# One load of x issued ahead of one load of addends, in a matmul kernel that streams its tiles

## Chip, cores and metric

The kernel runs on one core of a Trainium2 chip. The metric is the device time of one execution in microseconds (us), given as the median over several runs. The profile and the trace belong to one further execution, whose instructions and transfers the hardware profiler recorded.

## What is computed

```python
# x 16 x 512 x 1024, weight 1024 x 768, add_value 16 x 512 x 768, all float32; scale = 0.1
def reference(x, weight, scale, add_value):
    return (scale * np.matmul(x, weight) + add_value).astype(np.float32)
```

The 16 x 512 rows of x are one run of 8192 rows, that is 64 tiles of 128 rows. Each tile is multiplied by the same weight, scaled, and added to its tile of addends.

## The kernel before

**Data.** A group is eight tiles, and a partition of the chip holds eight neighbouring rows of a group, so that a load of four tiles of x brings 16 KB and a load of four tiles of addends 12 KB to each partition in one piece. `xs` has room for 16 tiles of x in float32 (a ring of four blocks of four tiles, one semaphore for each block: `x0` to `x3`). `ao` has room for 32 tiles: addends are loaded into it, the result is written over them, and the stores to `out` read it from there. The weight comes in through `ao` at the start and is kept as `w_bf` in bf16.

**Transfers.** All of them are issued by SyncE (SP) and go through one queue, in the order of the list `STREAM` (lines 19 to 25). An entry `("x", 56, 4)` loads four tiles of x from tile 56 on, `"a"` loads addends, `"w"` weights, and `"o"` stores results. `sync_engine` (lines 84 to 129) walks the list and puts a wait ahead of an entry only where it is needed, and only if no earlier wait on that semaphore was as strict (`need`, line 87):

- a load of x waits until ScalarE and GpSimd have cast the tiles that were in its place in the ring (lines 99 to 102);
- a load of addends that begins a group waits for the earlier such loads (line 109), and one into a place that held results waits for the store of these (line 114);
- a load of addends that begins in the middle of a group (tiles 52 to 55 are the only such load) signals `a_late`; all others signal `a_sem` (lines 116 to 120);
- a store waits for its results (`made`, line 125), and for the store two before it (line 124).

The last group of results (tiles 56 to 63, `LAST`) is stored by line 224, after all five engines have met at the end of the block that line 217 opens.

**Casting.** `mover` (lines 131 to 145) runs on ScalarE (ACT) and on GpSimd (POOL). For each block of four tiles it waits for the load, and for a free `va` buffer of the two, and then each engine makes eight casts of 32 partitions from `xs` to `va` (line 144). Blocks are taken in order.

**VectorE (DVE).** `group` (lines 172 to 179) is VectorE's fixed order for eight tiles. It mixes two kinds of work: `finish` takes the products of two tiles out of PSUM, scales them, adds the addends and leaves the result in `ao` (line 168); `turn` transposes half a cast block in 32 x 32 squares from `va` to `xt` (line 159). For tiles 48 to 55 the order is: wait for the addends of tiles 48 to 51; finish 48, 49; turn the first half of the block of tiles 52 to 55; finish 50, 51; turn its second half; **wait for `a_late`**; finish 52, 53; turn the first half of the block of tiles 56 to 59, which waits for all its casts; finish 54, 55; turn its second half. In the code:

```python
                if p == 2 and not last:
                    eng.wait_ge(a_late, i)
                finish(p, at, i + (4 * p - 12) if p < 3 else i)
                if p < 2 or not last:
                    turn(1 if p < 2 else 0, p % 2, i + 8 if p == 2 else i)
```

**TensorE (PE).** `tensor_engine` (lines 201 to 215) takes the tiles in order, sixteen matmuls a tile (eight slices of the contraction, each for 512 and 256 columns), into four PSUM places. Ahead of each pair of tiles it waits for their half block in `xt` and for the PSUM places to be finished.

## Time and profile before

The median of three runs is 212.03 us (211.53 to 212.54). The profiled execution took 212.22 us; its span, from the first to the last recorded instruction, is 210.2 us, and some 2.0 us lie around it.

| | busy us | share of the span | instructions |
|---|---|---|---|
| TensorE, matmuls (PE) | 170.3 | 81% | 1008 |
| TensorE, weight loads (PEld) | 50.8 | 24% | 512 |
| VectorE (DVE) | 97.9 | 47% | 66 |
| ScalarE (ACT) | 134.7 | 64% | 129 |
| GpSimd (POOL) | 135.4 | 64% | 132 |
| DMA queue | share of 16 engines 97.0% | 87.03 MB, mean 414 GB/s | 4720 packets |

The granted TensorE clock is 0.968 on average over the span. The DMA share is that of 16 DMA engines which work side by side: 1.00 says that all of them moved data all the time. A load or a store counts as landed when the last of the 16 engines has done its part. "Idle before" with an arrow names what ended an engine's wait. All stretches are in microseconds from the start of the span.

### The profile page before, as it was taken

What the parts mean: (1) busy time and instruction counts of PE and PEld (TensorE: products, weight loads), DVE (VectorE), ACT (ScalarE), POOL (GpSimd) and SP (SyncE); (2) the same over time, 40 slices, a digit from 0 to 9 for tenths busy, and PEclk for the clock granted to TensorE, in tenths of its full rate; (3) what the DMA queues carried; (4) which work ended last, traced back from release to release, by engine and by line L of the source; (5) the groups of instructions that cost most, each with busy time, mean ns of one, the idle gap of its engine ahead of it and who ended that gap; (6) DMA issues with size and microseconds to landing.
All of it is one profiled execution on the core that took longest, in us unless ns stands there. A gap on an engine that the chain in (4) does not pass through costs nothing.

```text
span 210.2 us, 2215 instructions
## 1 busy us (share of the span) xinstructions
PE 170.3 (81%) x1008; PEld 50.8 (24%) x512; DVE 97.9 (47%) x66; ACT 134.7 (64%) x129; POOL 135.4 (64%) x132
## 2 busy tenths in 40 slices
PE   0000999999999999999999999999998946999700
PEld 0000222223322223322223322223322211233200
DVE  0045245465537555555555555553719307155310
ACT  2492957995599999996950999379940599600000
POOL 0398956995599999997960899379950599700000
PEclk9999999999999999999999999999999995999985
DMA  6999999999999999999999999999999999999577
GB/s 231 407 447 447 412 426 424 449 449 399 455 443 399 424 474 399 449 426 412 435 421 437 451 421 441 418 426 449 402 426 433 430 449 430 416 430 444 234 299 299
DMA packets 4720, 87.03 MB, mean 414 GB/s; under 512 B 496, under 2 KB 496, under 8 KB 1008
## 3 DMA queue, kind: packets, MB, share of 16 engines
q1 hardware_dynamic: 4720, 87.03, 97.0%
HBM read 61.87 MB, written 25.17 MB: 414 GB/s over the span
## 4 chain that ended last, share of the span: by engine, by line
DMA 63%; POOL 15%; PE 11%; issue 2%; SPq 2%; DVE 1%; POOLq 0%; DVEq 0%
DMA xs<-in_x_dram 29%; DMA out_dram<-ao 27%; POOL va L144 15%; PE mm L193 11%; DMA ao<-in_add_value_dram 7%; DVE ao L168 1%; SPq L115 1%; DVE xt L159 1%; SPq L105 1%; SPq L96 0%; POOLq L137 0%; SPq L104 0%; POOLq L139 0%; SPq L89 0%; DVEq L157 0%
## 5 line engine op out<-in xcount | busy, mean ns | idle before, releaser
L193 PE MATMUL mm<-w_bf,xt 128*128 128x256 bf16 (+1 forms) x1008 | 170.3, 330 | 28.1 <-DVE xt L159 27.3
L144 POOL CAST va<-xs 32x1024 bf16<-32x1024 f32 x128 | 135.2, 1056 | 47.1 <-DMA xs<-in_x_dram 38.8
L144 ACT CAST va<-xs 32x1024 bf16<-32x1024 f32 x128 | 133.4, 1043 | 46.6 <-DMA xs<-in_x_dram 41.5
L168 DVE SCALAR_TENSOR_TENSOR ao<-mm,ao 128x1536 f32 (+1 forms) x32 | 56.2, 1755 | 75.6 <-PE mm L193 70.4
L191 PEld LDWEIGHTS <-xt 128*128 128x128 bf16 x512 | 50.8, 99 | 147.2 <-issue 118.3
L159 DVE STREAM_TRANSPOSE xt<-va 128x1024 f32<-128x1024 f32 x32 | 39.5, 1235 | 13.3 <-POOL va L144 13.3
L152 DVE CAST w_bf<-ao 128x3072 bf16<-128x3072 f32 x2 | 4.5, 2248 | 13.5 <-DMA ao<-in_weight_dram 13.5
L133 ACT ACT_TABLE_LOAD x1 | 1.3, 1283 | 0.9 <-SPq L217 0.9
L241 POOL MEMSET const-float32-0.0<- 128x1 f32 x1 | 0.1, 98 | 0.2 <-issue 0.2
L241 POOL MEMSET const-bfloat16-1.0<- 128x1 bf16 x1 | 0.1, 100 | 0.0
L241 POOL MEMSET const-float32-1.0<- 128x1 f32 x1 | 0.1, 98 | 0.0
L241 POOL MEMSET const-uint8-127<- 128x1 uint8 x1 | 0.1, 98 | 0.0
## 6 DMA issues: line engine op xcount, KB each, us to landing
out_dram<-ao SPq DMA_DIRECT2D x8, 3072.0 KB, 29.1
ao<-in_add_value_dram SPq DMA_DIRECT2D x7, 3072.0 KB, 17.1
xs<-in_x_dram SPq DMA_DIRECT2D x8, 2048.0 KB, 20.9
xs<-in_x_dram SPq DMA_DIRECT2D x4, 4096.0 KB, 23.1
ao<-in_weight_dram SPq DMA_DIRECT2D x2, 1536.0 KB, 12.3
ao<-in_add_value_dram SPq DMA_DIRECT2D x2, 1536.0 KB, 12.8
```

The lines of the kernel that those rows point to most:

```text
L105: move = eng.dma_start(xs[:, k:k + n, :], rows(x_v, s, n))
L115: move = eng.dma_start(ao[:, slot(s):slot(s) + n, :], rows(add_v, s, n))
L133: eng.preload_act_table(mybir.ActivationFunctionType.Copy)
L144: copy(va[q % VA_BUFS][32 * b:32 * b + 32, :, a, :], src[32 * a:32 * a + 32, :, b, :]).then_inc(count, 1)
L152: eng.tensor_copy(w_bf[:, s:s + n, :], ao[:, s:s + n, :]).then_inc(casts, n)
L159: eng.transpose(xt[:, 2 * half:2 * half + 2, :, :].rearrange("p i c m -> p (i c m)"), va[move % VA_BUFS][:, q:q + 2 * KC, :, :].bitcast(fp ...
L168: eng.scalar_tensor_tensor(a, mm[:, q:q + 2, 0:N], float(scale), a, op0=mybir.AluOpType.mult, op1=mybir.AluOpType.add).then_inc(made, 2)
L191: eng.ldweights(x_j, tile_position=(0, 0))
L193: m = eng.add_instruction(mybir.InstMatmult(start_tensor_calc=(j == 0), stop_tensor_calc=(j == KJ - 1), tile_size=(P, P), tile_position=(0 ...
L241: nc = _bacc.Bacc("TRN2", target_bir_lowering=False, num_devices=1)
```

## The change

One entry of the list moves ahead by one place. No instruction is added or removed.

```diff
@@ -20,8 +20,8 @@
     ("a", 24, 8), ("x", 32, 8), ("o", 0, 8), ("o", 8, 8), ("a", 32, 8), ("x", 40, 4),
-    ("x", 44, 4), ("a", 40, 8), ("x", 48, 8), ("o", 16, 8), ("o", 24, 8), ("a", 48, 4), ("a", 52, 4),
-    ("x", 56, 4), ("x", 60, 4), ("a", 56, 8), ("o", 32, 8), ("o", 40, 8), ("o", 48, 8),
+    ("x", 44, 4), ("a", 40, 8), ("x", 48, 8), ("o", 16, 8), ("o", 24, 8), ("a", 48, 4), ("x", 56, 4),
+    ("a", 52, 4), ("x", 60, 4), ("a", 56, 8), ("o", 32, 8), ("o", 40, 8), ("o", 48, 8),
 ]
 LAST = (56, 8)
```

In the built program only SyncE's order differs. Before, from the load of the addends of tiles 48 to 51 on: addends 48 to 51 (waits for the store of tiles 16 to 23), addends 52 to 55, x 56 to 59 (waits for casts), x 60 to 63 (waits for casts), addends 56 to 63, three stores. After: addends 48 to 51, x 56 to 59 (waits for casts), addends 52 to 55, x 60 to 63 (waits for casts), and the rest as before. The instructions of the other four engines, and their waits, are the same.

## The prediction

> **What bounds the kernel now.** I read the DMA share first, because 97.0% of 16 engines is the highest share on the page, and ask where the missing part is. The stretches of the last 45 us show it (columns: stretch, its length, busy time of PE, PEld, DVE, ACT, POOL with counts, granted clock, DMA share, GB/s):

> ```profile
> 170.40:172.50 2.10, 0.01 (x1) 0.00 (x0) 0.00 (x0) 2.05 (x3) 1.98 (x3) 1.00 1.01 433
> 172.50:175.40 2.90, 0.00 (x0) 0.00 (x0) 1.23 (x2) 2.83 (x4) 2.72 (x4) 0.54 0.95 407
> 175.40:179.70 4.30, 4.23 (x14) 1.06 (x8) 2.81 (x3) 4.20 (x5) 4.06 (x5) 0.51 1.05 452
> 179.70:196.20 16.50, 16.42 (x101) 4.95 (x51) 7.57 (x5) 2.50 (x3) 2.97 (x3) 1.00 1.00 429
> ...
> 197.30:198.00 0.70, 0.70 (x7) 0.20 (x3) 0.00 (x0) 0.00 (x0) 0.00 (x0) 1.00 0.10 35
> 198.00:198.50 0.50, 0.45 (x4) 0.00 (x0) 0.00 (x0) 0.00 (x0) 0.00 (x0) 1.00 0.12 49
> 198.50:201.00 2.50, 0.00 (x0) 0.00 (x0) 1.76 (x1) 0.00 (x0) 0.00 (x0) 1.00 0.00 0
> 201.00:208.90 7.90, 0.00 (x0) 0.00 (x0) 0.00 (x0) 0.00 (x0) 0.00 (x0) 0.66 0.93 398
> ```

> The queue is full until about 197.3, then nearly empty until 201, and then it moves the last store alone. So the hole of some 3.7 us ahead of the last store is all that the end of the kernel can give back. Next, the chain of waits (start, duration, what) says why the last store is late:

> ```profile
> 146.61 18.50 DMA xs<-in_x_dram
> ...
> 165.34 1.03 POOL va L144
> ...
> 174.17 1.26 DVE xt L159
> ...
> 175.47 10.30 PE mm L193 x50
> ...
> 198.56 1.76 DVE ao L168
> ```

> The load of x 56 to 59, issued at 146.61, lands at 165.1. Its casts, its transpose, the last eight tiles on TensorE and the last finish follow without a pause, and the store is issued at 200.60. The timeline shows TensorE's pause in it, and VectorE's order around that pause:

> ```profile
> 159.83 10.57 PE L193 MATMUL mm<-w_bf,xt 128*128 128x512 bf16 x63 [0.81 <-DVE xt L159]
> 175.47 22.98 PE L193 MATMUL mm<-w_bf,xt 128*128 128x512 bf16 x126 [5.07 <-DVE xt L159]
> 165.35 1.76 DVE L168 SCALAR_TENSOR_TENSOR ao<-mm,ao 128x1536 f32 x1 [2.79 <-PE mm L193]
> 174.17 1.25 DVE L159 STREAM_TRANSPOSE xt<-va 128x1024 f32<-128x1024 f32 x1 [7.06 <-POOL va L144]
> 156.92 28.19 SPq L126 DMA_DIRECT2D out_dram<-ao  x3
> ```

> TensorE ends tile 55 at 170.40 and starts tile 56 at 175.47. The finish of tiles 52 and 53 at 165.35, which needs the moved addends, waited for TensorE and not for them. (In the last row SyncE issues three stores, the third at 184.8, once the first has landed.)

> **The transfers one by one.** The rows of DMA issues, taken in stretches that hold one or two issues, give times to landing: addends 48 to 51, 11.2 us from 145.36, so 156.5; addends 52 to 55, 14.5 from 145.74, so 160.2; x 56 to 59, 165.1; x 60 to 63, 22.5 (the two x loads have a mean of 20.5, the first 18.5) from about 147.4, so 170.0; addends 56 to 63, 20.8 from 156.54, so 177.3; the stores of tiles 32 to 39 and 40 to 47, 27.8 and 34.8, so 184.7 and 192.2; the store of 48 to 55, 14.9 from 184.8, so 199.7. They land in the order of issue: a 3072 KB transfer takes 7.3 to 7.5 us of the ladder, x 4.9, the small addends 3.7.

> **The change, step by step.**

> *SyncE.* The same two DMAs swap places. The pair of addends took 1.15 us to issue, the pair of x 1.56, so x 56 is issued some 0.8 us earlier and addends 52 as much later. Both still stand in the queue behind the store of tiles 24 to 31 and addends 48, which land at 156.5, so this costs 0; without that cover it would be 0.8. The wait for casts that now comes ahead of addends 52 is for tiles 40 to 47 at most. POOL's timeline has its last 32 casts (tiles 48 to 63) from 138.00 on and the ones before ended at 133.5, 12 us before SyncE comes by: 0. What is queued behind it (x 60, addends 56, three stores) keeps its place, with the same bytes ahead.

> *x 56 to 59* lands behind addends 48 alone: 156.5 + 4.9 = 161.4 instead of 165.1, 3.7 earlier. From landing to TensorE's start took 175.47 - 165.11 = 10.36 (eight casts and a transpose). ACT and POOL are idle from 155.5 on, and VectorE has ended the finish of 52 and 53 by 167.1, so tile 56 starts at 161.4 + 10.4 = 171.8. TensorE's pause falls from 5.07 to 1.4.

> *Addends 52 to 55* land where x 56 did, at 165.1 (the sum of the bytes is the same), 4.9 later than before. Finish 52 needs them at 165.35, so the stall is 0 to 0.2. Behind that finish in VectorE's order stands the transpose of tile 56, which cannot start before its casts end at 170.4; the finish takes 1.76, so addends up to 168.4 cost nothing. Without that cover each microsecond is one.

> *x 60 to 63* lands at 170.0 as before. Its casts, so far hidden behind those of x 56 until 174.05, can now start at 170.4, take another 8.7 and end at 179.1. TensorE wants tile 60 four tiles (two finishes 5.2 apart, 188.16 to 193.36) after 171.8, at 182.2. With 1.3 for the transpose, 1.8 us are spare.

> *The clock.* The profile shows 1.00 after a pause of 0.81 us and about 0.5 from 172.7 to 179.7 around the pause of 5.07: the first pair of the last eight took 7.4 us, the later pairs 5.2. A pause of 1.4 lies between these rows, so 0 to 2.2 us can come on top of the 3.7. It is nearer the row of 0.81; but I carry both, since the last store is issued at 200.60 - 3.69 = 196.9 with the slow stretch, and at 194.7 without. [...]

> *The end.* Neither decides, because of the DMA queue. It has the same bytes to move before the last store: the store of tiles 48 to 55 is released by the landing at 184.7, which the swap does not touch, and lands at 199.7. Though most engines have done it by 198, 0.12 of 16 engines for 0.5 us at 198.0 to 198.5 is one engine with one more packet (a row counts a packet where it begins), and the last store cannot land before that engine has done its share of it too. Queued without a gap, it lands one more step of the ladder later: 199.7 + 7.5 = 207.2. Before it was 200.60 + 8.7 = 209.3. **Gain 2.1 us**, not 3.7. The condition is an issue before the late engine runs dry, at 199.2: with the 0.7 to 0.9 us from issue to first packet (issue at 200.60, none in 200.50 to 201.25, the first by 201.50) by 198.3. So 1.4 us are spare in the worse clock case, 3.6 in the better.

> **Sum.** Span 210.2 - 2.1 = 208.1, and with the same 2.0 around it 210.1 for the profiled execution. That one stood 0.19 above the median, so the forecast is 212.03 - 2.1 = **209.9 us**. Steps of 7.3 to 7.5 and the spread of the runs (0.5 to either side) give it a range of its own of 209.2 to 210.7.

> **Rivals.**

> *All of TensorE's gain comes through (chance 0.10).* If no engine is late on the store of 48 to 55, the last store starts at 197.5 and not at 201.3, the gain is 3.7, and the time 208.3. For it: the share is 0.10 already from 197.3 to 198.0. Against: the 0.12 after that, and the landing at 199.7.

> *The meeting of the engines waits for the store of 48 to 55 (0.08).* In the trace its landing, 199.7, comes before VectorE's end, 200.3, so it may be a hidden condition of line 224. Then the issue falls from 200.6 only to 199.7 + 0.3 = 200.0, a gain of 0.6: 211.4. Against: the list of SyncE's waits names VectorE alone there, and the code has no wait for these stores.

> *Slower: the addends of 52 come out of their turn (0.05).* Place: the wait for `a_late` in VectorE's order, ahead of the transpose that TensorE waits for. From the row of addends 48 (landing 156.5, finish 156.86, next transpose 158.54, TensorE 159.83), a landing at L starts tile 56 at L + 3.3. It decides from L = 168.5, the end moves when L passes 169.9, and above 172.2 the kernel is slower, one for one. With x 60 (170.0) nearly all the gain would remain; with addends 56 (177.3) tile 56 starts at 180.6, 5.1 late: 217.1. Against: every landing in the ladder is in order. [...]

> *The load does not come earlier (0.04).* If x 56 lands at 165.1 wherever it stands, nothing moves: 212.0. Against: the ladder again, where each transfer's step fits its bytes.

> **How the numbers follow.** My forecast has 0.73. About 0.5% (1.06 us) is what a measurement of this kernel can tell from no change, so faster means under 210.97: 0.72 of the forecast and the first rival, 0.82; the second, the fourth and a little of the forecast make 0.13 the same; 0.05 slower. The range reaches towards the first rival and down to a gain of 0.9: 208.6 to 211.1.

> **What would show it.** After: x 56 lands near 161.4 and TensorE's last pause is 1 to 2 us; the clock around it is 1.00, or dips; the finish of 52 still starts at 165.3 to 165.6; the third store is issued near 184.8; line 224 issues between 194 and 197.5; the DMA share has no hole ahead of the last store, whose time to landing grows from 8.7 to 10 or more; the end is near 208. Wrong would be: a last issue that waits for a landing, a VectorE wait on addends beyond 168, or a hole in the DMA share elsewhere.

## The result, and the profile after

The changed kernel takes 209.86 us (median), the kernel before beside it 212.41: a ratio of 0.9881, 95% interval 0.9854 to 0.9908, or 1.2% faster. One of the six runs of the changed kernel took 330.97 us at a mean granted clock of 0.566, for a reason that no run shows; the ratio leaves it out, and the median of the other five (209.78 to 209.94, clock 0.972 to 0.977) is 209.80. The profiled execution took 209.79 us, with a span of 207.7 us (before 212.22 and 210.2).

The issues of the two loads that changed places, from the rows of DMA issues (size, time to landing), in their new order:

```profile
xs<-in_x_dram SPq DMA_DIRECT2D x1, 2048.0 KB, 15.7
```

```profile
ao<-in_add_value_dram SPq DMA_DIRECT2D x1, 1536.0 KB, 18.5
```

Issued at 145.74 and 146.60, they land at 161.4 and 165.1; before, it was 165.1 and 160.2. The timeline of the changed kernel (start, duration, instruction; in brackets the idle time before it and what ended it):

```profile
171.77 20.98 PE L193 MATMUL mm<-w_bf,xt 128*128 128x512 bf16 x126 [1.37 <-DVE xt L159]
165.34 1.76 DVE L168 SCALAR_TENSOR_TENSOR ao<-mm,ao 128x1536 f32 x1 [2.79 <-PE mm L193]
170.47 1.25 DVE L159 STREAM_TRANSPOSE xt<-va 128x1024 f32<-128x1024 f32 x1 [3.36 <-POOL va L144]
177.37 1.76 DVE L168 SCALAR_TENSOR_TENSOR ao<-mm,ao 128x1536 f32<-128x1536 f32 x1 [2.87 <-DMA ao<-in_add_value_dram]
156.91 28.22 SPq L126 DMA_DIRECT2D out_dram<-ao  x3
194.89 0.33 SPq L224 DMA_DIRECT2D out_dram<-ao  x1
```

TensorE's pause ahead of tile 56 has gone from 5.07 to 1.37 us, and its last eight tiles run in 20.98 instead of 22.98. The finish of tiles 52 and 53 starts at 165.34 as before (165.35), so the later addends cost nothing there. Line 224 issues the last store at 194.89, 5.7 us earlier than before. Of these 5.7 the span has kept 2.5. The stretches show where the rest went (stretch, length, busy time of PE, PEld, DVE, ACT, POOL, granted clock, DMA share, GB/s):

```profile
170.40:172.50 2.10, 0.73 (x5) 0.29 (x3) 2.04 (x2) 2.05 (x3) 2.04 (x2) 1.00 1.04 445
172.50:175.40 2.90, 2.90 (x20) 0.88 (x9) 2.00 (x2) 2.83 (x4) 2.72 (x4) 1.00 0.97 415
175.40:179.70 4.30, 4.30 (x29) 1.27 (x13) 2.24 (x2) 3.10 (x3) 3.51 (x4) 1.00 1.04 446
...
197.30:198.00 0.70, 0.00 (x0) 0.00 (x0) 0.00 (x0) 0.00 (x0) 0.00 (x0) 0.50 1.23 527
198.00:198.50 0.50, 0.00 (x0) 0.00 (x0) 0.00 (x0) 0.00 (x0) 0.00 (x0) 0.50 0.80 344
198.50:201.00 2.50, 0.00 (x0) 0.00 (x0) 0.00 (x0) 0.00 (x0) 0.00 (x0) 0.50 0.96 413
```

The clock stays at 1.00 where it had been at 0.54 and 0.51. The hole of the DMA queue between 197.3 and 201 is filled. All five engines have ended their work by then: from about 195 on only the queue works. The times from issue to landing, of the store of tiles 48 to 55 (issued at 184.8) and of the last store:

```profile
DMA to landing us min/median/max: 14.8/14.8/14.8
```

```profile
DMA to landing us min/median/max: 11.9/11.9/11.9
```

That is 199.6 and 206.8. The last store stands in the queue for 11.9 us where it had taken 8.7, so 3.2 of the 5.7 us were paid there.

### The profile page after: what moved, and what is told of

It reads as the page before. It is cut to its first block, busy times and chain, and to the rows that moved or that the text cites. A ratio compares the mean times of both kernels' runs of the same rounds, so it can differ in the third digit from the quotient of the medians.

```text
span 207.7 us, 2215 instructions
## 1 busy us (share of the span) xinstructions
PE 168.2 (81%) x1008; PEld 50.4 (24%) x512; DVE 98.1 (47%) x66; ACT 134.7 (65%) x129; POOL 135.4 (65%) x132
## 3 DMA queue, kind: packets, MB, share of 16 engines
q1 hardware_dynamic: 4720, 87.03, 98.1%
## 4 chain that ended last, share of the span: by engine, by line
DMA 59%; POOL 15%; PE 10%; ACT 3%; issue 3%; DVE 1%; SPq 1%; POOLq 0%; DVEq 0%; ACTq 0%
DMA xs<-in_x_dram 41%; POOL va L144 15%; DMA out_dram<-ao 11%; PE mm L193 10%; DMA ao<-in_add_value_dram 7%; ACT va L144 3%; DVE ao L168 1%; DVE xt L159 1%; SPq L96 0%; SPq L105 0%; SPq L115 0%; POOLq L137 0%; SPq L104 0%; POOLq L139 0%; DVEq L157 0%
## 5 line engine op out<-in xcount | busy, mean ns | idle before, releaser
L193 PE MATMUL mm<-w_bf,xt 128*128 128x256 bf16 (+1 forms) x1008 | 168.2, 327 | 24.6 <-DVE xt L159 23.8
L144 POOL CAST va<-xs 32x1024 bf16<-32x1024 f32 x128 | 135.2, 1056 | 43.4 <-DMA xs<-in_x_dram 35.2
L144 ACT CAST va<-xs 32x1024 bf16<-32x1024 f32 x128 | 133.4, 1042 | 42.9 <-DMA xs<-in_x_dram 37.9
L168 DVE SCALAR_TENSOR_TENSOR ao<-mm,ao 128x1536 f32 (+1 forms) x32 | 56.2, 1755 | 72.7 <-PE mm L193 64.6
L159 DVE STREAM_TRANSPOSE xt<-va 128x1024 f32<-128x1024 f32 x32 | 39.5, 1235 | 10.3 <-POOL va L144 10.1
## 6 DMA issues: line engine op xcount, KB each, us to landing
ao<-in_add_value_dram SPq DMA_DIRECT2D x2, 1536.0 KB, 14.9
```

What stands on the lines that cost most here:

```text
L144: copy(va[q % VA_BUFS][32 * b:32 * b + 32, :, a, :], src[32 * a:32 * a + 32, :, b, :]).then_inc(count, 1)
L159: eng.transpose(xt[:, 2 * half:2 * half + 2, :, :].rearrange("p i c m -> p (i c m)"), va[move % VA_BUFS][:, q:q + 2 * KC, :, :].bitcast(fp ...
L168: eng.scalar_tensor_tensor(a, mm[:, q:q + 2, 0:N], float(scale), a, op0=mybir.AluOpType.mult, op1=mybir.AluOpType.add).then_inc(made, 2)
L193: m = eng.add_instruction(mybir.InstMatmult(start_tensor_calc=(j == 0), stop_tensor_calc=(j == KJ - 1), tile_size=(P, P), tile_position=(0 ...
```

## The experiments

**Where the rest of TensorE's gain is.** Two kernels do without the store of tiles 48 to 55, so that the queue has run empty when the last store is issued: once from the kernel before, once from the changed one.

```diff
-    ("a", 52, 4), ("x", 60, 4), ("a", 56, 8), ("o", 32, 8), ("o", 40, 8), ("o", 48, 8),
+    ("a", 52, 4), ("x", 60, 4), ("a", 56, 8), ("o", 32, 8), ("o", 40, 8),
```

> The kernel before, without the store of tiles 48 to 55 (these rows are left out). Theory: its last store is set by TensorE's chain and found an empty queue anyway, so nothing changes: issue at 200.6, end of the span 210.2, 212.0 to 212.4 us. Rival (the meeting of the engines or the end of the program waits for that store): the last store is issued earlier, by up to 0.6.

> The changed kernel, without the store of tiles 48 to 55 (these rows are left out). Theory: the queue is empty when line 224 issues at 194.9, so the last store lands 8.7 later at 203.6 and the span ends at 204.5: all of TensorE's gain (3.7 of the pause, 2.0 of the clock) shows, 5.7 us against the same kernel without the change, about 206.5 us. Rival (TensorE gained only what the time shows): 209.8, as with that store.

Measured: 212.35 us without the change (ratio to the kernel before 0.9995, 0.9973 to 1.0018), and 206.86 us with it (0.974, 0.9711 to 0.9768). Taking 3072 KB from the queue gives the kernel before nothing, since it was not waiting for them, and gives the changed kernel another 3.0 us. Between the two medians lie 5.5 us, and between the two profiled executions 5.8 (212.62 and 206.77): all that TensorE gained. From the timelines, first the one without the change:

```profile
175.45 23.39 PE L193 MATMUL mm<-w_bf,xt 128*128 128x512 bf16 x128 [5.07 <-DVE xt L159]
200.98 0.33 SPq L224 DMA_DIRECT2D out_dram<-ao  x1
```

```profile
172.01 20.97 PE L193 MATMUL mm<-w_bf,xt 128*128 128x512 bf16 x128 [1.39 <-DVE xt L159]
195.14 0.33 SPq L224 DMA_DIRECT2D out_dram<-ao  x1
```

Of the 5.8 us between the two issues, 3.4 come from the earlier start of tile 56 and 2.4 from the clock (23.39 against 20.97 for the same 128 matmuls). In both kernels the last store then lands 8.7 us after its issue. The meeting of the engines did not wait for the store that was left out: in the kernel before, line 224 issues 0.28 us after VectorE's last finish with that store (198.56 + 1.76, then 200.60) and without it (198.94 + 1.76, then 200.98).

**How much is spare.** Transposes that nothing needs are put on VectorE behind its last finish; each waits for the one before.

```diff
         group(2 * T, slice(s, s + 1), True)
+        for j in range(2):
+            eng.wait_ge(turned, TURNED + T + 2 * j)
+            eng.transpose(
+                xt[:, 2:4, :, :].rearrange("p i c m -> p (i c m)"),
+                va[1][:, 2 * KC:4 * KC, :, :].bitcast(fp32).rearrange("p c a k -> p (c a k)"),
+            ).then_inc(turned, 2)
```

> The changed kernel once more, as the measure for the runs beside it. Theory: 209.8 to 210.0 us, with a smaller spread from run to run than the kernel before (its end hangs on the count of bytes, not on when a load landed and where the clock stood).

> The changed kernel with two more transposes on VectorE behind the last finish, which nothing needs: the last store is issued 2.5 to 2.8 us later, at about 197.6. Theory (3.5 us to spare before the DMA queue runs dry on its last engine): no change, 209.9 us within 0.3. Rival (TensorE's and VectorE's chain sets the end): 2.5 to 2.8 us longer, 212.5.

> The changed kernel with six more transposes on VectorE behind the last finish: the last store is issued 7.5 to 8.2 us later, at about 202.7. Theory (the first 3.5 to 4 us are free, the rest counts): the store lands 8.7 after its issue, at 211.4, against 206.8: 4.6 us longer, 214.4 us, between 214 and 215. Rival (nothing is spare): 7.5 to 8.2 longer, 217.7.

> The kernel before with two more transposes on VectorE behind the last finish. Theory (nothing is spare before the change): 2.5 to 2.8 us longer than the kernel before, 214.7 to 215.2 us. Rival (the queue hides as much there): no change.

The changed kernel was timed once more beside them, without added work.

| kernel | median us | ratio to before (95%) |
|---|---|---|
| changed | 209.96 | 0.9886 (0.9861 to 0.9911) |
| changed, two more | 210.03 | 0.9891 (0.9866 to 0.9916) |
| changed, six more | 214.59 | 1.0108 (1.0074 to 1.0141) |
| before | 212.34 | |
| before, two more | 214.84 | 1.0106 (1.0079 to 1.0132) |

The changed kernel with two and with six more, and the kernel before with two more:

```profile
194.68 2.58 DVE L191 STREAM_TRANSPOSE xt<-va 128x1024 f32<-128x1024 f32 x2
197.55 0.33 SPq L230 DMA_DIRECT2D out_dram<-ao  x1
DMA to landing us min/median/max: 9.4/9.4/9.4
```

```profile
194.59 7.99 DVE L191 STREAM_TRANSPOSE xt<-va 128x1024 f32<-128x1024 f32 x6
202.86 0.33 SPq L230 DMA_DIRECT2D out_dram<-ao  x1
DMA to landing us min/median/max: 8.7/8.7/8.7
```

```profile
201.43 2.59 DVE L191 STREAM_TRANSPOSE xt<-va 128x1024 f32<-128x1024 f32 x2
204.30 0.33 SPq L230 DMA_DIRECT2D out_dram<-ao  x1
DMA to landing us min/median/max: 8.7/8.7/8.7
```

The same 2.6 us of work cost 2.5 us before the change (214.84 against 212.34) and 0.07 after it. Issued at 197.55, the last store takes 9.4 us instead of 11.9: what is lost in front of it comes back in the queue. By then nearly all of the DMA engines have run dry (the DMA share is 0.10 from 197.3 to 198.0), and yet the end comes no later.

```profile
197.30:198.00 0.70, 0.00 (x0) 0.00 (x0) 0.00 (x0) 0.00 (x0) 0.00 (x0) 0.50 0.10 35
```

The trace has a signal of each of the 16 DMA engines for every landing. Here fifteen have done the last store by 206.2, that is 8.7 us after its issue, as from an empty queue; the last signal comes at 207.0, which is 7.3 after the last signal of the store ahead of it (199.7). So it is the late engine, and not the issue, that sets this end. With 8.0 us of work it takes 8.7, the queue is empty, and 4.6 us show (214.59 against 209.96), for now the store comes too late for that engine as well. So about 3.4 us (8.0 less 4.6) were free, which agrees with the 3.6 worked out for the clock's better case.

**What the addends cost if they come later still.** The load of addends 52 to 55 is moved one and two places further back.

```diff
-    ("a", 52, 4), ("x", 60, 4), ("a", 56, 8),
+    ("x", 60, 4), ("a", 52, 4), ("a", 56, 8),
```

```diff
-    ("a", 52, 4), ("x", 60, 4), ("a", 56, 8),
+    ("x", 60, 4), ("a", 56, 8), ("a", 52, 4),
```

> The addends of tiles 52 to 55 are loaded one place later still, behind x 60 to 63. Theory (the DMA queue sets the end, TensorE has some 3.5 us to spare): these addends land at 170.0, VectorE finishes tiles 52 and 53 at 170.3 instead of 165.3, TensorE starts tile 56 at 173.3 instead of 171.8 (the landing plus 3.3), the last store is issued 1.5 us later than after the change, or up to 3.7 later if the clock falls, and still finds a queue that is not empty: 209.9 us, within 0.4. Rival (TensorE's chain sets the end after the change too): 1.5 to 3.7 us longer, 211.4 to 213.6.

> The addends of tiles 52 to 55 are loaded two places later still, behind the addends of tiles 56 to 63. Theory (landings come in the order of issue, and the transpose of tile 56 stands behind the finish of tiles 52 and 53 in VectorE's order): they land at 177.3, TensorE starts tile 56 at 180.6 at half clock, the last store is issued at 205.7 into an empty queue: 5.1 us slower than before, 217.1 to 217.5 us. Rival (landings are not bound to the order of issue, or the wait is hidden): about 210.

Measured: 209.9 us one place back (0.9881, 0.9859 to 0.9904), 217.16 us two places back (1.023, 1.0198 to 1.0263). The timelines, one place back and then two:

```profile
170.15 1.76 DVE L168 SCALAR_TENSOR_TENSOR ao<-mm,ao 128x1536 f32 x1 [7.66 <-DMA ao<-in_add_value_dram]
173.12 20.97 PE L193 MATMUL mm<-w_bf,xt 128*128 128x512 bf16 x128 [2.78 <-DVE xt L159]
196.24 0.33 SPq L224 DMA_DIRECT2D out_dram<-ao  x1
```

```profile
177.43 1.76 DVE L168 SCALAR_TENSOR_TENSOR ao<-mm,ao 128x1536 f32 x1 [14.95 <-DMA ao<-in_add_value_dram]
180.40 22.60 PE L193 MATMUL mm<-w_bf,xt 128*128 128x512 bf16 x128 [10.07 <-DVE xt L159]
205.14 0.33 SPq L224 DMA_DIRECT2D out_dram<-ao  x1
```

In both, VectorE stands at the wait for `a_late`, and TensorE starts tile 56 some 3 us after that finish begins: at 173.12 and 180.40, where the landing plus 3.3 had given 173.3 and 180.6. One place back TensorE is 1.35 us later than in the changed kernel, and it costs nothing, for the queue has that much to spare. Two places back all of the rest is used up, and the kernel is 4.7 us slower than before the change (217.16 against 212.5). The slower rival's mechanism is real; in this change its condition was not met. The moved addends landed at 169.9 and 177.2, where 170.0 and 177.3 had been worked out from the bytes ahead of them.

## Why the prediction was right

- **x 56 to 59 3.7 us earlier.** Predicted landing 161.4 and start of tile 56 at 171.8; measured 161.4 and 171.77. Right.
- **Addends 52 to 55 at no cost.** Predicted landing 165.1 against a need at 165.35; measured 165.1, and the finish did not move. In the experiment one place back it moved by 4.8 us, to 170.15, and the time did not change, so slack stands behind it.
- **x 60 to 63 in time.** Predicted end of its casts 179.1, measured 179.1 (GpSimd, 161.64 + 17.45); the transpose that needs it began at 179.2, and TensorE went from tile 56 to the end without a pause.
- **The clock.** Left open between 0 and 2.2 us; measured 0 after a pause of 1.37. In the one profile of the experiment one place back it stayed full after 2.78 too. The last section says why that need not hold in every run.
- **The end.** The step that mattered was that the DMA queue takes over and passes on only part of TensorE's gain. The run without the store of tiles 48 to 55 and the added transposes show it from two sides. Predicted landing 207.2, measured 206.8: the store of tiles 48 to 55 landed 0.1 earlier, and the last step took 7.2 us, not 7.5. So the gain of 2.1 was sized a little small; the medians give 2.4 to 2.6.
- **The forecast time** (209.9 against 209.86) is closer than its parts: it started from a median of 212.03 for the kernel before, which with more runs is 212.3 to 212.5, and the gain was taken too small by about as much. Two errors of some 0.4 us cancelled, and that is luck.
- **Rivals.** That all of TensorE's gain comes through (208.3) needed a store of tiles 48 to 55 on which no engine is late. In the changed kernel fifteen engines had done that store by 198.4 and the last one at 199.6, and the last store by 205.6 and 206.8, so the condition was not met. That the meeting of the engines waits for the store of tiles 48 to 55 is refuted by the issue at 194.89, before that store landed. That x 56 to 59 does not land earlier is refuted by its landing at 161.4. The rival of a slower kernel is the subject of the last experiment.
- **Missed.** The finish of tiles 56 and 57 now waits for its own addends: 2.87 us idle, ended by a DMA at 177.37, where the products were due at 177.0. The working followed x 60 to 63 and the addends of 52, but not the load behind them. It cost some 0.4 us on VectorE and nothing at the end. Taken by its words, this is one of the prediction's signs of being wrong, "a VectorE wait on addends beyond 168"; the working behind that sign was about the addends of tiles 52 to 55, which did not make VectorE wait.

No kernel run here that does all the work is clearly faster than the changed one. Its DMA share is 98.1% of the span.

## What to carry to other kernels

Where one queue is full from start to end but for a hole ahead of the last transfer (here 3.7 us), the hole is the most that a better order of that end can give, whatever the compute engines gain (here 5.7 us, of which the span kept 2.5): work out when the queue would run dry on its last engine, not when most engines do. Swapping two loads in this full queue moved each by the time of the other's bytes (x 3.7 us earlier, the addends 4.9 later), so both landings could be worked out from neighbours. Each has to be held against the first instruction that needs it and against what stands behind that instruction on its engine.

## What the runs showed of the hardware

The run to run spread of the kernel before goes with TensorE's clock. After a pause of 5.07 or 5.08 us its last eight tiles took 22.98, 23.39 and 23.85 us in three profiles (of the kernel before, of the one without a store, of the one with two more transposes), after one of 10.07 us 22.60, and after pauses of 1.37 to 2.78 us 20.97 or 20.98 each time. In the runs of the kernel before beside the experiments, those with a mean granted clock of 0.974 or 0.975 took 211.6 to 212.0 us, those with 0.961 or 0.962 took 212.6 to 213.3. The kernels with a short pause spread little in the runs of the experiments: 209.76 to 210.09 for the changed one, 206.77 to 207.1 for the one whose last store found an empty queue, so this is not the DMA queue's doing.

One of the 16 DMA engines ran late. In the profile before, it still had a packet to begin in the stretch 198.0 to 198.5 (one packet, a DMA share of 0.12) when the others had none left: the fifteenth signal of that store came at 198.35, the last at 199.68. The last landing signal came 0.04 us behind the fifteenth for the first load, 0.24 for the addends that landed at 110.9, 0.75 for those at 156.5, and 1.33 for the store that landed at 199.7; for the last store, issued into an empty queue, it was 0.01. The signals do not name the engine. No run evened out the engines' shares, so what that would bring stays open.

Whole transfers of 1536 to 4096 KB landed in the order of their issue: all 31 in the profile before, and all 31 in the profile after.
